# Attention rows split pair by pair, small loads on another queue, and a last block in two tiles

## The chip, the cores and the metric

The kernel runs on one core of one Trainium2 chip. The metric is the device time of one execution in microseconds. Before the change three runs took 2020.02, 2020.78 and 2021.38 us.

## The reference

The reference is an encoder trunk of two layers on x of 256 rows by 2048 columns, all in float32. Cut to what matters:

```
for l in range(DEPTH):
    h = rms_norm(x, norm1_g[l])
    q, k, v, gu, gv = jnp.split(h @ w_in[l], splits, axis=-1)
    q = apply_rope(rms_norm(q.reshape(B, S, N_Q_HEADS, HEAD_DIM), q_norm_g[l]), cos, sin)
    k = apply_rope(rms_norm(k.reshape(B, S, N_KV_HEADS, HEAD_DIM), k_norm_g[l]), cos, sin)
    attn = banded_window_attention(q, k, v, sink[l])
    sgu = chunked_spatial_gating(jax.nn.gelu(gu), jax.nn.gelu(gv), sgu_ln_g[l], sgu_ln_b[l], w_s[l], b_s[l])
    mixed = jnp.concatenate([rms_norm(attn, attn_out_g[l]), rms_norm(sgu, sgu_out_g[l])], axis=-1)
    x = x + mixed @ w_o[l]
    x = x + conv_gated_ffn(rms_norm(x, norm2_g[l]), w_up[l], conv_w[l], conv_b[l], w_down[l])
```

There are 8 query heads and 2 key heads of 128 columns, a gating unit of 1024 columns, and a feed-forward width of 5632.

## The kernel before, in words

**Products in three parts.** Every float32 factor is split into a high part (rounded to the matmul's fp32r type) and a low part (the rest). A product is high by high, high by low and low by high. `split_weights` (L112) asks for 1 MB of weights on SP's queue into one of three `raw` buffers; ScalarE copies a half of it (1024 columns) into one of four `hi` buffers (L128), and VectorE subtracts to one of four `lo` buffers (L110). Activations are split the same way into a `sl` tile of two parts: with a gain per row by `split_act` (ScalarE L246, VectorE L247), without one by `split_plain` or `parts` (L260, L261). `sl` tiles come from a pool of 43.

**Two forms of products.** `rows_by_cols` (L160) makes 256 rows by 512 columns of a result, in two halves `m` of 128 rows: 24 products of 512 columns for each 1 MB of weights (L166), six for each of four blocks of 128 rows of weights. `unit` (L187) makes columns by rows: 32 products of 512 (L202) and 32 of 256 columns (L207) for 2 MB. `pair` (L213) does this for two units of the feed-forward part (L225, L231). Results lie in PSUM: three `mm` tiles of two banks, and two `tp` tiles of one bank for transposes, scores and attention values.

**A layer.** First the keys, values and the first four query heads (`psk`, `psq`), four blocks of weights each; then `chunk(1)`, the second four query heads; `chunk(3)` and `chunk(4)`, the gating values; then four gating units (`gated`), the output projection (`out_rows`: four column blocks over the attention rows, four over the gating rows), and the feed-forward part in two halves of the width.

**The attention** is a Python generator, `attend` (L392), one for each group of four heads. Its steps are called between the weight blocks of the chunks, so that its small products stand among the large ones: rotation and norm of the queries; their transposes (L410); scores (L266 to L268 through `matmul3`), mask (L422), maximum and exp (L441); then for each pair of heads the scaling of the probabilities (L453), their transposes (L459), and the value product (L266 to L268 again). Its result is copied to an `sl` tile (L467) and its squares are added to `acca` (L277); the tile goes into a list `att`. After the first gating unit, L676 splits all eight rows of this list with the gain of the attention norm.

**What sets the order.** The code is written in the order of the work, and a scheduler moves instructions by priorities; `urgent()` puts weight splits and a few others ahead. Each engine then does its instructions in one fixed order, and waits at each for what it needs. `let_in` places the transposes of a norm (L320: the first norm `r1` as rows) behind 8 products of the block that runs then, and `tc.issue_after(latest())` lets nothing in it stand ahead of the instruction that was the latest of TensorE.

**The small loads.** In layer 0 the x rows that are split for the first products come on SP's queue between the weights, pair by pair (L515, `first_rows`). Ahead of the last block, x for the residual (`xr`, 2 MB in two loads, L554), the gains `qk`, the rest of the columns `pc` and `ropes` are asked for on SP's queue. The sum of squares of `xr` gives the first norm `r1` (L306, L310, L281, L283). In each layer `gating_tables` (L356) asks for two loads of `wsT` and six broadcasts of `prow` right after the first queries.

**Start and end.** `WARM` products of a tile of ones run ahead of the first weights (L97). The last column block of the last layer is added to the residual and stored from one `mm` tile: the weights' last 1 MB is run first for the one half of the rows, then for the other (`apart`), and L772 and L773 add and store one half whole and the other in two parts, on SP's queue.

Of the kernel before, what the change touches and what calls it, by code (L numbers as in the profile page):

```python
# [8 lines left out]
F32 = mybir.dt.float32  # L9
# [5 lines left out]
P = 128  # L15
# [15 lines left out]
WARM = 10  # L31
# [9 lines left out]
def encoder(ctx: ExitStack, tc: tile.TileContext, xT, x, w_in, w_gu, w_o, w_up, w_down, wsT, pcol, prow, rope, out):  # L41
# [106 lines left out]
    def latest():  # L148
        return next(i for i in reversed(nc.cur_bb.bb.instructions) if i.engine == mybir.EngineType.PE)
# [10 lines left out]
    def rows_by_cols(ps, acts, src, first, last, raw=None, apart=False):  # L160
        his, los = split_weights(src, raw)

        def product(m, kk, part):
            cs = slice(kk % 2 * W, (kk % 2 + 1) * W)
            w = (his if part < 2 else los)[kk // 2][:, cs]
            nc.tensor.matmul(  # L166
                ps[:, m, :], acts[kk][:, part % 2, m * P : (m + 1) * P], w,
                start=first and kk == 0 and part == 0, stop=last and kk == KB - 1 and part == 2,
            )

        if apart:
            for m in range(2):
                for kk in range(KB):
                    for part in range(3):
                        product(m, kk, part)
            return
        for kk in range(KB):
            for m in range(2):
                product(m, kk, 0)
                product(m, kk, 1)  # L180
            for m in range(2):
                product(m, kk, 2)
            if kk == 1:
                let_in()
# [207 lines left out]
    def attend(g, ps, r, kT, v, tab, qk, nsink, acc, outs):  # L392
# [55 lines left out]
        for pr in range(2):  # L448
# [20 lines left out]
            outs.append(o)  # L469
        yield  # L470


    def gained(tiles, g0, pc):
        return [split_act(t[:, i, :], pc[:, g0 + 2 * j + i : g0 + 2 * j + i + 1]) for j, t in enumerate(tiles) for i in range(2)]
# [48 lines left out]
    def residual(ps, c, r=None):  # L523
        with urgent():
            for m in range(2):
                to = xr[:, m, c * W : (c + 1) * W]
                if r is None:
                    nc.vector.tensor_tensor(out=to, in0=ps[:, m, :], in1=to, op=ALU.add)
                else:
                    nc.vector.scalar_tensor_tensor(  # L530
                        out=to, in0=ps[:, m, :], scalar=r[:, m : m + 1], in1=to, op0=ALU.mult, op1=ALU.add
                    )
# [4 lines left out]
    for l in range(DEPTH):  # L537
# [10 lines left out]
        for b in range(NB):  # L548
            if l == 0:
                first_rows(b)  # L550
            if b == NB - 1:
                if l == 0:
                    for m in range(2):
                        nc.sync.dma_start(xr[:, m, :], x[:, m, :])  # L554
# [7 lines left out]
            in_rows(psk, 2, b)  # L562
            in_rows(psq, 0, b)
        r1b = as_rows(r1)
        ws, lrows = gating_tables(l)
        acca = sl([P, 2, SEQ])
        att = []
# [26 lines left out]
        def chunk(c, steps):  # L594
            ps = mm()
# [4 lines left out]
            return ps  # L600

        def group_steps(g, ps):
            it = attend(g, ps, r1, kT, vs, tabs[0], qk, nsink, acca, att)
# [7 lines left out]
        second()  # L611

# [63 lines left out]
        atts = gained(att, C_AG, pc)  # L676
# [18 lines left out]
        def out_rows(half, c, r):  # L695
            ps = mm()
# [37 lines left out]
        for f0, f1 in ((0, 24), (24, NF)):  # L734
# [20 lines left out]
            for c in range(4):  # L755
                ps = mm()
                end = last and not more and c == 3
                for k in range(f0, f1, KB):
# [8 lines left out]
                for m in range(2):  # L767
                    step = W // 2 if end and m else W
                    for a in range(0, W, step):
                        to = xr[:, m, c * W + a : c * W + a + step]  # L770
                        with urgent():
                            nc.vector.tensor_tensor(out=to, in0=ps[:, m, a : a + step], in1=to, op=ALU.add)  # L772
                        nc.sync.dma_start(out[:, m, c * W + a : c * W + a + step], to)  # L773
# [57 lines left out]
```

## Time and profile before

| what | value |
|---|---|
| median of three runs | 2020.78 us |
| the profiled execution, its own time | 2020.79 us |
| its span | 2019.0 us |
| mean granted clock of TensorE | 0.998 |
| instructions | 26362 |
| DMA, mean | 189 GB/s |

The span is what the profiler saw, from the first to the last instruction; the execution's own time is 1.8 us longer. In the timeline a row has its start, its length, the engine, line and operation, out<-in, and the number of instructions merged; in brackets stands the idle time of the engine ahead of it and what ended it. PE is TensorE's products, PEld its weight loads, SPq and ACTq the queues' DMA issues. The lengths of overlapping instructions overlap, so the pitch of a merged row is what counts.

### The profile page before, as it was taken

To read this page: it belongs to the slowest core of one execution; us is meant where nothing else is said; L and a number is where in the kernel's file an instruction comes from. 1 tells how busy PE (TensorE), PEld (TensorE's weight loads), DVE (VectorE), ACT (ScalarE), POOL (GpSimd) and SP (SyncE) were. 2 spreads that over 40 slices of the span, in tenths; PEclk is the share of its full clock that TensorE was granted. 3 is DMA by queue.
4 is the path that set the end of the run, shared out by engine and by line. 5 is a ranking of instruction groups with operands and counts; after the bars stand their busy time and mean duration, and the time that the engine had idled before them with its cause. 6 is when DMAs were issued, how large, how long until landed. Compare 5 with 4: busy or idle time off the path is not lost.

```text
span 2019.0 us, 26362 instructions
## 1 busy us (share of the span) xinstructions
PE 2003.4 (99%) x10428; PEld 1719.2 (85%) x10428; DVE 1367.1 (68%) x1866; ACT 1066.3 (53%) x1459; POOL 19.2 (1%) x25
## 2 busy tenths in 40 slices
PE   9998999999999999999999999999999999999999
PEld 7787888888888888888888888888988888888887
DVE  6787666777765477776558696667777554777753
ACT  5665465555543365555445754655555434555542
POOL 0000000000000000000001000000000000000000
PEclk9999999999999999999999999999999999999999
DMA  8643554554565454456565445454555555455563
GB/s 325 236 137 135 188 167 167 212 186 167 205 215 193 164 209 182 167 211 209 186 230 184 149 157 197 158 198 167 188 210 199 195 194 182 167 191 206 209 210 124
DMA packets 58011, 382.22 MB, mean 189 GB/s; under 512 B 6688, under 2 KB 7968, under 8 KB 12832
## 3 DMA queue, kind: packets, MB, share of 16 engines
q1 hardware_dynamic: 57744, 380.53, 53.3%
q8 instruction: 81, 1.33, 0.3%
q14 instruction: 42, 0.34, 0.1%
q10 hardware_dynamic: 144, 0.02, 0.0%
HBM read 378.43 MB, written 2.10 MB: 188 GB/s over the span
## 4 chain that ended last, share of the span: by engine, by line
PE 93%; DVE 1%; ACT 0%; DMA 0%; issue 0%; POOL 0%; DVEq 0%; ACTq 0%; SPq 0%
PE mm L166 39%; PE mm L225 30%; PE mm L231 16%; PE mm L202 4%; PE mm L207 2%; DVE lo L110 1%; PE tp L501 1%; PE tp L266 0%; PE tp L648 0%; DMA raw<-in_w_up 0%; PE tp L268 0%; PE tp L267 0%; PE tp L459 0%; ACT hi L128 0%; DVE sl L261 0%
## 5 line engine op out<-in xcount | busy, mean ns | idle before, releaser
L110 DVE TENSOR_TENSOR lo<-raw,hi 128x1024 fp32r<-128x1024 f32 (+1 forms) x708 | 840.0, 1214 | 461.4 <-ACT hi L128 303.2
L128 ACT ACTIVATE hi<-raw 128x1024 fp32r<-128x1024 f32 (+1 forms) x708 | 732.6, 1051 | 683.4 <-PE mm L166 396.0
L166 PE MATMUL mm<-hi,sl 128*128 128x512 f32 x2560 | 692.9, 391 | 6.1 <-DVE sl L247 5.3
L225 PE MATMUL mm<-sl,hi 128*128 128x512 f32 x2688 | 617.5, 389 | 0.1
L225 PEld LDWEIGHTS mm<-sl,hi 128*128 128x128 f32 x2688 | 501.9, 188 | 103.0 <-ACT hi L128 0.5
L166 PEld LDWEIGHTS mm<-hi,sl 128*128 128x128 f32 x2560 | 478.9, 188 | 105.0 <-DVE sl L247 6.3
L166 PE MATMUL mm<-lo,sl 128*128 128x512 f32 x1280 | 395.8, 390 | 0.0
L231 PEld LDWEIGHTS mm<-sl,lo 128*128 128x128 f32 x2688 | 328.1, 192 | 3.3
L231 PE MATMUL mm<-sl,lo 128*128 128x256 f32 x2688 | 329.1, 283 | 0.0
L166 PEld LDWEIGHTS mm<-lo,sl 128*128 128x128 f32 x1280 | 240.4, 188 | 50.1
L726 DVE SCALAR_TENSOR_TENSOR sc<-ev,pc,sc 128x255 f32<-128x255 f32 x176 | 80.7, 480 | 87.9 <-ACT sc L725 87.9
L239 ACT COPY ev<-mm 128x512 f32<-128x512 f32 x96 | 55.4, 577 | 131.6 <-PE mm L231 114.8
L725 ACT ACTIVATE sc<-ev,pc 128x256 f32<-128x256 f32 x176 | 98.9, 589 | 0.0
L202 PE MATMUL mm<-sl,hi 128*128 128x512 f32 x384 | 92.4, 392 | 0.0
L202 PEld LDWEIGHTS mm<-sl,hi 128*128 128x128 f32 x384 | 70.9, 188 | 13.9
L729 DVE SCALAR_TENSOR_TENSOR sc<-ev,pc,sc 128x255 f32<-128x255 f32 x176 | 80.7, 480 | 3.0
L254 ACT ACTIVATE sl<-sl 128x256 fp32r<-128x256 f32 x88 | 31.8, 409 | 69.2 <-DVE sl L746 69.2
L241 DVE TENSOR_TENSOR ev<-mm,ev 128x512 f32<-128x512 f32 x96 | 65.4, 682 | 0.0
L721 DVE TENSOR_TENSOR ev<-ev,rb 128x512 f32<-128x512 f32 x88 | 59.9, 681 | 0.2
L207 PE MATMUL mm<-sl,lo 128*128 128x256 f32 x384 | 50.5, 284 | 0.0
L207 PEld LDWEIGHTS mm<-sl,lo 128*128 128x128 f32 x384 | 48.4, 191 | 1.0
L255 DVE TENSOR_TENSOR sl<-sl 128x256 fp32r<-128x256 f32 x88 | 33.4, 421 | 20.1 <-ACT sl L254 20.1
(117 smaller groups left out, 633.1 us busy)
## 6 DMA issues: line engine op xcount, KB each, us to landing
raw<-in_w_up SPq DMA_DIRECT2D x176, 1024.0 KB, 5.2
raw<-in_w_down SPq DMA_DIRECT2D x88, 1024.0 KB, 4.8
raw<-in_w_in SPq DMA_DIRECT2D x38, 1024.0 KB, 4.9
raw<-in_w_o SPq DMA_DIRECT2D x32, 1024.0 KB, 4.9
raw<-in_w_gu SPq DMA_DIRECT2D x16, 1024.0 KB, 4.9
sl<-in_prow SPq DMA_DIRECT2D x12, 256.0 KB, 5.7
raw<-in_w_in SPq DMA_DIRECT2D x8, 256.0 KB, 5.8
xr<-in_x SPq DMA_DIRECT2D x2, 1024.0 KB, 7.6
```

Source lines behind the costliest of these rows:

```text
L110: nc.vector.tensor_tensor(out=lo, in0=part, in1=hi.bitcast(F32), op=ALU.subtract)
L128: nc.scalar.activation(hi[:, cs], part, AF.Copy)
L166: nc.tensor.matmul(ps[:, m, :], acts[kk][:, part % 2, m * P : (m + 1) * P], w, start=first and kk == 0 and part == 0, stop=last and kk == ...
L202: nc.tensor.matmul(ps[:, i, :], tile_of(his, k, i), x1, start=k == 0, stop=False)
L207: nc.tensor.matmul(ps[:, i, :SEQ], tile_of(los, k, i), acts[k][:, 0, :], start=False, stop=k == NK - 1)
L225: nc.tensor.matmul(pss[n][:, i, :], hs[k // KB][:, c : c + P], x1, start=k == 0, stop=False)
L231: nc.tensor.matmul(pss[n][:, i, :SEQ], los[k // KB][:, c : c + P], acts[k][:, 0, :], start=False, stop=k == len(acts) - 1)
L241: nc.vector.tensor_tensor(out=s, in0=ps[:, :, :SEQ], in1=rest, op=ALU.add)
L721: nc.vector.tensor_tensor(out=s, in0=s, in1=r2b2[0], op=ALU.mult)
L725: nc.scalar.activation(t[:, i, :], s[:, i, :], AF.Identity, bias=col(3), scale=col(1))
L726: nc.vector.scalar_tensor_tensor(out=t[:, i, 1:], in0=s[:, i, : SEQ - 1], scalar=col(0), in1=t[:, i, 1:], op0=ALU.mult, op1=ALU.add)
L729: nc.vector.scalar_tensor_tensor(out=t[:, i, : SEQ - 1], in0=s[:, i, 1:], scalar=col(2), in1=t[:, i, : SEQ - 1], op0=ALU.mult, op1=ALU.add)
```

## The change

It has five parts.

- `attend` splits a pair of attention rows right where it has made them (L470 to L473 of before), with `gained`, and appends the split rows to `atts`; the splitting of all eight after the first gating unit is gone.
- In layer 0 the loads of `ropes`, `qk` and the rest of `pc` are issued from ScalarE's queue in the second block, and the two loads of `xr` in the third; each stands behind the instruction that was ScalarE's latest then.
- `gating_tables` is called after the first step of the second query group instead of ahead of the keys.
- The last column block gets two `tp` tiles of one bank, one for each half of the rows, and the store of the last 256 columns is issued from ScalarE's queue. For this `ps` is now a list of two halves in every caller.
- `WARM` is 9 instead of 10.

```
-WARM = 10
+WARM = 9
...
-    def attend(g, ps, r, kT, v, tab, qk, nsink, acc, outs):
+    def gained(tiles, g0, pc):
+        return [split_act(t[:, i, :], pc[:, g0 + 2 * j + i : g0 + 2 * j + i + 1]) for j, t in enumerate(tiles) for i in range(2)]
+
+    def attend(g, ps, r, kT, v, tab, qk, nsink, acc, pc, outs):
...
             add_squares(acc, o, g == 0 and pr == 0)
-            outs.append(o)
+            outs.extend(gained([o], C_AG + 4 * g + 2 * pr, pc))
...
                 first_rows(b)
+
+                with tc.issue_after(latest(mybir.EngineType.Activation)):
+                    if b == 1:
+                        ropes = const.tile([P, 2, 2, HD], F32, tag="ropes", name="ropes")
+                        nc.scalar.dma_start(ropes, rope)
+                        qk = layer_params_rest(0, pc, nc.scalar)
+                    if b == 2:
+                        for m in range(2):
+                            nc.scalar.dma_start(xr[:, m, :], x[:, m, :])
             if b == NB - 1:
                 if l == 0:
-                    for m in range(2):
-                        nc.sync.dma_start(xr[:, m, :], x[:, m, :])
                     for c in range(4):
                         sum_squares(ssq, c)
-                    qk = layer_params_rest(0, pc, nc.sync)
-                    ropes = const.tile([P, 2, 2, HD], F32, tag="ropes", name="ropes")
-                    nc.sync.dma_start(ropes, rope)
...
         r1b = as_rows(r1)
-        ws, lrows = gating_tables(l)
...
         second()
+        ws, lrows = gating_tables(l)
...
         gated(0)
-        atts = gained(att, C_AG, pc)
...
-                ps = mm()
                 end = last and not more and c == 3
+                ps = [tp([P, W]) for _ in range(2)] if end else (lambda t: [t[:, m, :] for m in range(2)])(mm())
...
-                        nc.sync.dma_start(out[:, m, c * W + a : c * W + a + step], to)
+                        (nc.scalar if end and a else nc.sync).dma_start(out[:, m, c * W + a : c * W + a + step], to)
```

The scheduler moves more than the diff says. SP's queue at the start, before (`raw` are weights, `sl<-in_xT` the x rows to be split, `xr` the residual's x):

```order
L118 DMA raw<-in_w_in 128x2048
L515 DMA sl<-in_xT 128x512
L118 DMA raw<-in_w_in 128x2048 x2
L515 DMA sl<-in_xT 128x512
L118 DMA raw<-in_w_in 128x2048
L515 DMA sl<-in_xT 128x512
```

and the same place after:

```order
L515 DMA sl<-in_xT 128x512
L118 DMA raw<-in_w_in 128x2048
L515 DMA sl<-in_xT 128x512
L118 DMA raw<-in_w_in 128x2048 x2
L515 DMA sl<-in_xT 128x512
L118 DMA raw<-in_w_in 128x2048
```

Each load of x rows now stands ahead of the weights that it stood behind.

TensorE between the transposes of the first group's queries (L410, in after L414; `ident` is the unit matrix) and its first scores (L266), before:

```order
L410 MATMUL tp<-ident,sl 128x128 x4
L166 MATMUL mm<-hi,sl 128x512 x2
L166 MATMUL mm<-lo,sl 128x512 x2
L166 MATMUL mm<-hi,sl 128x512 x4
L266 MATMUL tp<-sl 128x256
```

and after:

```order
L414 MATMUL tp<-ident,sl 128x128 x8
L166 MATMUL mm<-hi,sl 128x512 x4
L166 MATMUL mm<-lo,sl 128x512 x2
L166 MATMUL mm<-hi,sl 128x512 x4
L166 MATMUL mm<-lo,sl 128x512 x2
L166 MATMUL mm<-hi,sl 128x512 x4
L166 MATMUL mm<-lo,sl 128x512 x2
L166 MATMUL mm<-hi,sl 128x512 x4
L166 MATMUL mm<-lo,sl 128x512 x2
L266 MATMUL tp<-sl 128x256
```

Eight products stood between them, and 24 do now.

VectorE ahead of layer 0's output projection, before (L241 and L638 join and scale a gating unit, L277 adds squares, L247 splits, L288 and L296 sum the attention's squares):

```order
L110 TENSOR_TENSOR lo<-raw,hi 128x1024 x3
L241 TENSOR_TENSOR ev<-mm,ev 128x512
L110 TENSOR_TENSOR lo<-raw,hi 128x1024
L638 TENSOR_TENSOR ev<-ev,rb 128x512
L277 TENSOR_TENSOR sl<-sl,sc 128x512
L247 SCALAR_TENSOR_TENSOR sl<-sl,pc 128x256 x8
L288 TENSOR_TENSOR sl<-sl 128x256
L296 TENSOR_REDUCE as<-tp 128x2
```

and after (L643 is L638 of before):

```order
L643 TENSOR_TENSOR ev<-ev,rb 128x512
L277 TENSOR_TENSOR sl<-sl,sc 128x512
L247 SCALAR_TENSOR_TENSOR sl<-sl,pc 128x256 x2
L261 TENSOR_TENSOR sl<-tp,sl 128x512 x2
L277 TENSOR_TENSOR sl<-sl,sc 128x512
L288 TENSOR_TENSOR sl<-sl 128x256
L247 SCALAR_TENSOR_TENSOR sl<-sl,pc 128x256
L296 TENSOR_REDUCE as<-tp 128x2
L247 SCALAR_TENSOR_TENSOR sl<-sl,pc 128x256
```

The eight splits in a row are gone; those of the last two pairs are left here, two behind the one sum, and one each around the sums for the norm.

More of the change, by code (lines that the diff above doesn't have):

```diff
@@ L145, in split_later, with latest @@
         return los
-    def latest():
-        return next(i for i in reversed(nc.cur_bb.bb.instructions) if i.engine == mybir.EngineType.PE)
+    def latest(engine=mybir.EngineType.PE):
+        return next(i for i in reversed(nc.cur_bb.bb.instructions) if i.engine == engine)
     waiting = []
@@ L166, in product @@
             nc.tensor.matmul(
-                ps[:, m, :], acts[kk][:, part % 2, m * P : (m + 1) * P], w,
+                ps[m], acts[kk][:, part % 2, m * P : (m + 1) * P], w,
                 start=first and kk == 0 and part == 0, stop=last and kk == KB - 1 and part == 2,
@@ L468, in attend @@
             add_squares(acc, o, g == 0 and pr == 0)
-            outs.append(o)
+            outs.extend(gained([o], C_AG + 4 * g + 2 * pr, pc))
         yield
-    def gained(tiles, g0, pc):
-        return [split_act(t[:, i, :], pc[:, g0 + 2 * j + i : g0 + 2 * j + i + 1]) for j, t in enumerate(tiles) for i in range(2)]
     qk = None
@@ L550, in encoder @@
                 first_rows(b)
+                with tc.issue_after(latest(mybir.EngineType.Activation)):
[6 more added lines that the diff above has]
+                            nc.scalar.dma_start(xr[:, m, :], x[:, m, :])
             if b == NB - 1:
                 if l == 0:
[L553 to L554 removed]
                     for c in range(4):
                         sum_squares(ssq, c)
[L557 to L559 removed]
                 tabs, nsink = rope_tables(qk, ropes)
                 r1 = inv_rms_rows(ssq, "x")
[L562 to L563 removed]
+            in_rows([psk[:, m, :] for m in range(2)], 2, b)
+            in_rows([psq[:, m, :] for m in range(2)], 0, b)
         r1b = as_rows(r1)
[L565 removed]
         acca = sl([P, 2, SEQ])
[L567 removed]
+        atts = []
         kms = st([P, 2, 2], "kms")
@@ L594, in chunk @@
         def chunk(c, steps):
-            ps = mm()
+            t = mm()
+            ps = [t[:, m, :] for m in range(2)]
             for b in range(NB):
@@ L599, in chunk @@
                     step()
-            return ps
+            return t
         def group_steps(g, ps):
-            it = attend(g, ps, r1, kT, vs, tabs[0], qk, nsink, acca, att)
+            it = attend(g, ps, r1, kT, vs, tabs[0], qk, nsink, acca, pc, atts)
             return lambda: next(it)
@@ L695, in out_rows @@
         def out_rows(half, c, r):
-            ps = mm()
+            t = mm()
+            ps = [t[:, m, :] for m in range(2)]
             for b in range(2):
```

7 lines of the change are left out of this document (3 added, 4 removed).

## Prediction

> **What bounds the kernel now.** I read the page first, its busy times and the chain that ended last.
>
> ```profile
> PE 2003.4 (99%) x10428; PEld 1719.2 (85%) x10428; DVE 1367.1 (68%) x1866; ACT 1066.3 (53%) x1459; POOL 19.2 (1%) x25
> PE 93%; DVE 1%; ACT 0%; DMA 0%; issue 0%; POOL 0%; DVEq 0%; ACTq 0%; SPq 0%
> 1253.20 10.93 PE mm L166 x48
> ```
>
> TensorE is busy for 2003.4 of the span's 2019.0 us and holds 93% of the chain. A weight product of 512 columns takes 10.93 / 48 = 0.228 us (the third line, from the chain in order of time). The change removes one tiny warm-up product and no other, so it can only move the places where TensorE stands still. So I went through the timeline of PE alone, from start to end, for rows that begin with an idle time:
>
> ```profile
> 9.40 1.20 PE L166 MATMUL mm<-hi,sl 128*128 128x512 f32 x4 [0.77 <-ACT hi L128]
> 59.62 0.43 PE L320 MATMUL tp<-ident,xr 128*128 128x128 f32 x2 [0.74 <-POOL xr L283]
> 95.34 0.38 PE L266 MATMUL tp<-sl 128*128 128x256 f32 x1 [1.05 <-DVE sl L261]
> 105.28 0.36 PE L266 MATMUL tp<-sl 128*128 128x256 f32 x1 [1.41 <-DVE sl L422]
> 135.97 0.66 PE L459 MATMUL tp<-ident,sl 128*128 128x128 f32 x4 [0.23 <-DVE sl L261]
> 189.92 1.65 PE L166 MATMUL mm<-hi,sl 128*128 128x512 f32 x3 [5.30 <-DVE sl L247]
> 1165.98 0.47 PE L266 MATMUL tp<-sl 128*128 128x512 f32 x1 [0.40 <-DVE sl L261]
> ```
>
> All but the last lie in layer 0, and one is larger than all others together. It also costs more than its length, as the view by windows shows (after the engines' busy times come the granted clock, the DMA share and GB/s):
>
> ```profile
> 190.00:192.00 2.00, 2.00 (x5) 1.61 (x6) 2.00 (x6) 0.00 (x0) 0.00 (x0) 0.50 0.91 377
> 192.00:193.60 1.60, 1.60 (x6) 0.97 (x6) 0.97 (x3) 0.00 (x0) 0.00 (x0) 0.50 0.26 108
> 193.60:195.00 1.40, 1.40 (x14) 1.40 (x14) 0.87 (x3) 0.00 (x0) 0.47 (x1) 0.97 0.00 0
> ```
>
> After the pause TensorE runs at half clock from 189.92 to 193.60, so 3.68 x 0.5 = 1.8 us are lost on top. The shorter pauses are not followed by this.
>
> **Part 1, the attention splits.** What TensorE waited for at 189.92 is all eight splits in one row:
>
> ```profile
> 183.04 3.50 DVE L110 TENSOR_TENSOR lo<-raw,hi 128x1024 fp32r<-128x1024 f32 x3 [5.24 <-ACT hi L128]
> 183.18 1.69 ACT L246 ACTIVATE sl<-sl,pc 128x256 fp32r<-128x256 f32 x4
> 184.23 0.39 PE L166 MATMUL mm<-hi,sl 128*128 128x512 f32 x1
> 189.40 3.24 DVE L247 SCALAR_TENSOR_TENSOR sl<-sl,pc 128x256 fp32r<-128x256 f32 x8
> ```
>
> The chain in order of time has the price of the gating unit's half-length products:
>
> ```profile
> 1293.15 3.83 PE mm L207 x32
> ```
>
> TensorE was at the output projection at 184.23, but VectorE had stood idle for 5.24 us and then did low weight parts, a join and a sum first. A split of one pair costs ScalarE 2 x 1.69 / 4 = 0.85 us and VectorE 2 x 3.24 / 8 = 0.81 us. After the change three pairs are split long before, and only the last pair's two stand near the projection; by the order of VectorE they come ahead of the gating's sums. Between the last pair's value product and the projection TensorE has 4 big and 32 half-length products, 4 x 0.228 + 3.83 = 4.7 us, and the projection's first 24 products read the other group's pairs, 5.5 us more. In these 10.2 us ScalarE has a copy, a square, a high weight part and two splits to do, and VectorE two sums and two splits; at no more than 1.06 us each for the first three (the length of a high part, in a row below) that is 3.2 + 0.85, and 0.4 for the last split, 4.4 us. So the pause goes: 5.3 + 1.8 = **7.1 us**. If the cover failed, 7.1 would come back.
>
> What is put ahead of something else: each pair's 0.85 and 0.81 us stand before the next pair's copies and low parts, for which TensorE waits (the rows at 95.34, 135.97 and 1165.98 are this kind of wait). Between the first transposed probabilities and the first value product TensorE now has 8 products in layer 0 and 7 in layer 1, where it had 11 and 14: 1.8 and 1.6 us. Per place I bound the wait by 0 (the copies land in time) and 1.41 (the largest such row); four first pairs make 0 to 5.6. The two waits nearest to this in kind took 0.23 and 0.40, so I take 0.25 for each place, **1.0 us** in all, and count those two old waits as staying.
>
> **Part 2, the small loads.** Today the residual x is asked for on SP's queue, between weight loads:
>
> ```profile
> 42.38 0.42 SPq L554 DMA_DIRECT2D xr<-in_x  x1
> 57.08 0.62 ACT L306 ACTIVATE sc<-xr 128x512 f32<-128x512 f32 x1
> 57.60 0.19 ACT L306 ACTIVATION_READ_ACCUMULATOR sc<-xr 128x1 f32 x1
> 58.86 0.71 POOL L283 TENSOR_TENSOR xr<-xv,mhalf 128x2 f32<-128x2 f32 x1 [56.63 <-DVE xv L281]
> ```
>
> Its second half is asked for at 42.38, so the last square ends at 57.79 and the norm at 59.57, and the transposes of L320 wait 0.74. Now ScalarE asks for x one block of 48 products, 10.9 us, earlier in the program. The scheduler put L320's transposes after 204 products in place of 227: from 17.69 (48 products done) that is 17.69 + 156 x 0.228 = 53.3. The last two squares stand behind a high part whose buffer frees 38 products before its own use, about product 178, 47.3 us; with 1.06 for the part, two squares at 0.62 + 0.19 and the 1.8 from the last square to the norm that it took before, it is ready near 51.8. Gain **0.7**.
>
> The early norm moves what follows. Between the queries' transposes and the first scores stand 24 products, not 8: the 1.05 wait needed 8 x 0.228 + 1.05 = 2.9 us and gets 5.5. Between those and the third score stand 61, not 30: needed 6.8 + 1.41 = 8.2, given 13.9. Gain **2.5**.
>
> Against it: each of five loads takes ScalarE about 0.42 us of issue, and other loads meet them.
>
> ```profile
> 50.53 1.06 ACT L128 ACTIVATE hi<-raw 128x1024 fp32r<-128x1024 f32 x1 [1.66 <-PE mm L166]
> raw<-in_w_in SPq DMA_DIRECT2D x38, 1024.0 KB, 4.9
> xr<-in_x SPq DMA_DIRECT2D x2, 1024.0 KB, 7.6
> ```
>
> ScalarE waits 1.66 us before each high part because the buffer isn't free, not for the load; that hides 0.42 us each, and the 36 products of buffers ahead hide more. An x load of 1 MB beside a weight load of 1 MB took 7.6 where 4.9 is usual, so I bound the delay by 2.7 us per half, 5.4 in all, and take 0. The Trainium skill ("DMA: Bandwidth & Descriptors", section "Issuing engines are not separate DMA queues") says that all queues feed the same 16 DMA engines, so a second queue adds no bandwidth; by it alone x would hold back a weight load as before, and the sum would lose up to those 5.4 us if no cover stood there.
>
> The gating tables go behind the second queries' weights, past eight weight loads of 24 products each at the most:
>
> ```profile
> 59.79 0.65 SPq L364 DMA_DIRECT2D sl<-in_prow  x1
> 135.83 0.68 DVE L667 TENSOR_TENSOR vn<-vn,sl 128x512 f32<-128x512 f32 x1
> ```
>
> Asked for from 59.79 + 8 x 5.5 = 104 on, they are there long before their first reader at 135.83: nothing, and the weight loads that they stood before come a little sooner, into full buffers.
>
> **Part 3, the start.**
>
> ```profile
> 1.05 4.63 PE L97 MATMUL tp<-ones 128*128 128x128 f32 x20 [1.05 <-DVE ones L93]
> 5.34 1.46 PE L166 MATMUL mm<-hi,sl 128*128 128x512 f32 x4
> 8.71 0.63 ACT L128 ACTIVATE hi<-raw 128x512 fp32r<-128x512 f32 x1 [1.07 <-DMA raw<-in_w_in]
> 12.71 0.63 ACT L128 ACTIVATE hi<-raw 128x512 fp32r<-128x512 f32 x1 [0.36 <-DMA raw<-in_w_in]
> 15.30 1.06 ACT L128 ACTIVATE hi<-raw 128x1024 fp32r<-128x1024 f32 x1 [1.95 <-DMA raw<-in_w_in]
> 16.33 1.07 PE L166 MATMUL mm<-hi,sl 128*128 128x512 f32 x4
> 17.69 1.36 PE L166 MATMUL mm<-hi,sl 128*128 128x512 f32 x4
> ```
>
> One warm-up product of ten (two passes of twenty) is 0.46 us. The first real product, at 5.34, can come that much earlier, but the third piece of weights lands at 8.71 whatever TensorE does, and the start at 9.40 stays: nothing. The Trainium skill ("TensorE: Matmul & The Clock Gate", section "Part 1: The HAM clock gate (the "warmup" mystery)") says that the clock starts at half and rises after some 3.4 us of activity, whatever the number of products; if the shorter warm-up missed that window, the twelve products before 9.40 at double length would take 5.5 us from 4.9 and end at 10.4, a loss of 1.0 us by estimate. The sum goes by the rows: nothing.
>
> Then SP asks for the second pair of x rows (0.25 MB) ahead of the next weights. 1 MB took 15.30 - 12.71 = 2.6 us, so the weights land 0.65 later, at 15.95, and their high part ends at 17.0, before TensorE asks at 17.69. In return these x rows are split before they are needed: the four products at 17.69 took 1.36 us against the usual 1.07, and the next x rows can do the same once more. Gain **0.4** of the 0.3 to 0.6; if the weights came after 17.69 instead, the end is a loss of as much.
>
> **Part 4, the end.**
>
> ```profile
> 2011.31 0.39 PE L166 MATMUL mm<-lo,sl 128*128 128x512 f32 x1
> 2014.45 1.35 DVE L772 TENSOR_TENSOR xr<-mm,xr 128x512 f32<-128x512 f32 x3 [9.02 <-PE mm L166]
> 2015.17 1.31 SPq L773 DMA_DIRECT2D out_x<-xr  x3
> L772 DVE TENSOR_TENSOR xr<-mm,xr x9: 414/680/692, 1932.9 to 2015.4; 128x512 f32<-128x512 f32 x7, 128x256 f32<-128x256 f32 x2
> L773 SPq DMA_DIRECT2D out_x<-xr x9: 332/343/446, 1933.6 to 2016.0; - x9
> DMA to landing us min/median/max: 1.9/2.1/2.1
> ```
>
> The first half of the rows is done at 2011.70 but is added only at 2014.45, since both halves are one tile. In two tiles it is added and stored beside the second half's products. Then two halves of 0.414 us, overlapping to 0.34 apart, end at 2015.20, and the last store starts at 2015.24 on ScalarE's queue, not at 2016.0: **0.7 us**. If a store from that queue landed later, 0 to 0.7.
>
> **The sum.** 7.1 + 0.7 + 2.5 + 0.4 + 0.7 - 1.0 = 10.4 us. The profiled execution took 2020.79, its span 2019.0 and 1.8 around it; the median of the runs is 2020.78, the same. Forecast **2010.4 us**.
>
> **The rivals.** (1) *The hand-offs eat a part.* With 7 and 8 products of cover, each of the four first pairs waits 1.0 to 1.4 us: 3 to 4.6 more than I took, 2013.4 to 2015. For it: the rows at 95.34 and 105.28; against: the copies are ordered right behind the transposes. (2) *The projection still pauses.* Something else at the end of VectorE's row, such as the last pair, holds it for 5.30 and the clock halves: 7.1 back, 2017.5, no change that can be told. (3) *Slower.* The pause that halves the clock moves into the hand-offs: VectorE, held by a low part that waits for its buffer as it was for 5.24 us, lets TensorE stand long enough there. Each is worth 7.1; two cancel the gain (2024.6), from three on it is slower: 2031.7. Against it, no hand-off paused over 1.41. (4) *The early x holds back weights* at the start, against full buffers: 5.4 at most, 2013 to 2015.8.
>
> **Chances.** About 0.2%, 4 us, is what a measurement of this kernel can tell from no change: faster is below 2016.8, slower above 2024.8. Forecast 0.62; (1) 0.14; (4) 0.06; (2) 0.10; (3) 0.04; 0.04 unnamed, half of it faster, half the same. Faster 0.84, same 0.12, slower 0.04. The range goes from all waits gone (the sum without the 1.0 and with 0.23 and 0.40 gone too: 2008.8, less 0.3 for spread) to the ends of (1) and (4): **2008.5 to 2016.0**.
>
> **What would show it.** Right: no idle time over 1 us before a product of L166 near 180 us and a granted clock of 1.00 there; no wait at L320; scores without waits of 1.05 and 1.41; the last store starting near 2005 and 0.7 us sooner after the last product. Wrong: rows of L266 or of the probabilities' transposes with idle times over 1 us, in layer 1 above all, or a high part that waits for DMA between 20 and 50 us and a product that waits for it.

## The result, and the profile after

The changed kernel takes 2008.41 us (median of 6 runs, 2008.03 to 2008.88), the kernel before 2020.33 (6 runs, 2019.68 to 2021.38): a ratio of 0.9941, 95% interval 0.9928 to 0.9954. The gain is 11.9 us where 10.4 were forecast, and the time lies 0.09 below the low end of the range. The profiled execution took 2008.75, its span 2007.0, so the two spans differ by 12.0.

The page's busy times and the chain that ended last, of the changed kernel:

```profile
PE 2000.7 (100%) x10426; PEld 1718.6 (86%) x10426; DVE 1367.1 (68%) x1866; ACT 1068.1 (53%) x1460; POOL 20.4 (1%) x25
PE 97%; DMA 2%; DVE 1%; issue 0%; ACT 0%; SPq 0%; POOL 0%; DVEq 0%; ACTq 0%
```

These are its rows of PE with an idle time ahead of them, from start to end, and the view by windows of the stretch that had the pause:

```profile
42.14 1.48 PE L166 MATMUL mm<-hi,sl 128*128 128x512 f32 x4 [0.65 <-ACT sl L246]
137.22 0.39 PE L266 MATMUL tp<-sl 128*128 128x256 f32 x1 [0.21 <-DVE sl L426]
177.49 0.41 PE L294 MATMUL tp<-ident,sl 128*128 128x128 f32 x2 [0.16 <-DVE sl L288]
1158.63 1.25 PE L463 MATMUL tp<-ident,sl 128*128 128x128 f32 x8 [0.40 <-DVE sl L457]
126.00:200.00 74.00, 73.62 (x420) 64.17 (x419) 63.31 (x109) 48.85 (x80) 1.39 (x2) 1.00 0.42 143
```

The pause of 5.30 us is gone, with the waits at L320, at the scores (1.05, 1.41) and at 9.40; the granted clock is 1.00. New are a wait for x rows at 42.14 and two short ones. Idle time ahead of PE's rows, as the profile lists it, fell from 10.95 to 2.48 us, 1.05 of it ahead of the first product in both.

The transposes of a norm (L320) stand four times in TensorE's order and make milestones. These are the last three before, then all four after:

```profile
300.27 0.38 PE L320 MATMUL tp<-ident,yr 128*128 128x128 f32 x2
1064.49 0.38 PE L320 MATMUL tp<-ident,xr 128*128 128x128 f32 x2
1299.57 0.38 PE L320 MATMUL tp<-ident,yr 128*128 128x128 f32 x2
```

```profile
53.44 0.38 PE L320 MATMUL tp<-ident,xr 128*128 128x128 f32 x2
288.42 0.38 PE L320 MATMUL tp<-ident,yr 128*128 128x128 f32 x2
1052.64 0.38 PE L320 MATMUL tp<-ident,xr 128*128 128x128 f32 x2
1288.23 0.38 PE L320 MATMUL tp<-ident,yr 128*128 128x128 f32 x2
```

The first of them stands 23 products (5.2 us) earlier in the order than before, so 5.2 is added to it and taken from the stretch behind it:

| stretch | before | after | difference | forecast |
|---|---|---|---|---|
| start to first norm | 59.62 | 58.65 | -1.0 | -1.1 (0.7 + 0.4) |
| to layer 0's second norm | 240.65 | 229.8 | -10.9 | -9.1 (7.1 + 2.5 - 0.5) |
| to layer 1's first norm | 764.22 | 764.22 | 0 | 0 |
| to layer 1's second norm | 235.08 | 235.59 | +0.5 | +0.5 |
| to the last product's end | 714.85 | 715.10 | +0.25 | 0 |
| to the span's end | 4.58 | 3.67 | -0.9 | -0.7 |

The end of the changed kernel, in the timeline:

```profile
2000.65 0.69 DVE L777 TENSOR_TENSOR xr<-tp,xr 128x512 f32<-128x512 f32 x1 [6.29 <-PE tp L166]
2002.94 0.39 PE L166 MATMUL tp<-lo,sl 128*128 128x512 f32 x1
2003.37 0.76 DVE L777 TENSOR_TENSOR xr<-tp,xr 128x256 f32<-128x256 f32 x2 [2.03 <-PE tp L166]
2004.15 0.35 ACTq L778 DMA_DIRECT2D out_x<-xr  x1
```

The first half is added while the second is multiplied, and the last store starts 0.8 us behind the last product's end at 2003.33, where it was 1.6 behind before.

### The profile page after: what moved, and what is told of

Same layout as the page of the kernel before. It is cut to its first block, busy times and chain, and to the rows that moved or that the text cites. A ratio compares the mean times of both kernels' runs of the same rounds, so it can differ in the third digit from the quotient of the medians.

```text
span 2007.0 us, 26356 instructions
## 1 busy us (share of the span) xinstructions
PE 2000.7 (100%) x10426; PEld 1718.6 (86%) x10426; DVE 1367.1 (68%) x1866; ACT 1068.1 (53%) x1460; POOL 20.4 (1%) x25
## 4 chain that ended last, share of the span: by engine, by line
PE 97%; DMA 2%; DVE 1%; issue 0%; ACT 0%; SPq 0%; POOL 0%; DVEq 0%; ACTq 0%
PE mm L166 40%; PE mm L225 30%; PE mm L231 16%; PE mm L202 4%; PE mm L207 2%; PE tp L166 1%; DMA raw<-in_w_in 1%; PE tp L501 1%; DMA sl<-in_xT 1%; PE tp L463 0%; PE tp L266 0%; PE tp L653 0%; DVE lo L110 0%; PE tp L268 0%; PE tp L267 0%
## 5 line engine op out<-in xcount | busy, mean ns | idle before, releaser
L166 PE MATMUL mm<-hi,sl 128*128 128x512 f32 x2480 | 668.0, 391 | 0.7 <-ACT sl L246 0.7
L166 PEld LDWEIGHTS mm<-hi,sl 128*128 128x128 f32 x2480 | 463.9, 188 | 96.4 <-ACT sl L246 1.1
L166 PE MATMUL mm<-lo,sl 128*128 128x512 f32 x1240 | 382.9, 390 | 0.0
L166 PEld LDWEIGHTS mm<-lo,sl 128*128 128x128 f32 x1240 | 232.5, 188 | 48.1
L241 DVE TENSOR_TENSOR ev<-mm,ev 128x512 f32<-128x512 f32 x96 | 65.7, 684 | 0.0
```

Of the source, the lines that this page charges most:

```text
L166: nc.tensor.matmul(ps[m], acts[kk][:, part % 2, m * P : (m + 1) * P], w, start=first and kk == 0 and part == 0, stop=last and kk == KB - 1 ...
L241: nc.vector.tensor_tensor(out=s, in0=ps[:, :, :SEQ], in1=rest, op=ALU.add)
```

## The experiments

The theory to test is the forecast's own: the splits by pairs remove the pause, the earlier loads remove the waits at L320 and at the scores, the tables do nothing. The rival is that one wait has several removers among the parts, so that their gains don't add.

**The parts one at a time.** The splits alone, put into the kernel before:

```
-            outs.append(o)
+            outs.extend(gained([o], C_AG + 4 * g + 2 * pr, pc))
...
-        atts = gained(att, C_AG, pc)
```

> The kernel before with one part of the change alone: each pair of attention rows is split where it is made. Theory A: the pause of 5.30 us near 185 us goes with its 1.8 us of halved clock, and up to 0.4 us of new waits at the hand-offs comes: 2020.3 - 7.1 + 0.4 = 2013.6 us, 2013.0 to 2014.2; the other waits (0.77, 0.74, 1.05, 1.41) stay. Rival B (the other parts made the gain): 2018 to 2020. Rival C (with the transposes where they were, the hand-offs have less cover and wait 1.0 us each at four places): 2015 to 2017.

Measured: 2013.92 us (2013.60 to 2015.17; before on the same chip 2020.46), ratio 0.9969 (0.9958 to 0.9981): 6.5 less. A holds. The pause is gone, the score waits stay, and the hand-offs take more in layer 1:

```profile
94.75 0.39 PE L266 MATMUL tp<-sl 128*128 128x256 f32 x1 [1.02 <-DVE sl L261]
104.67 0.36 PE L266 MATMUL tp<-sl 128*128 128x256 f32 x1 [1.41 <-DVE sl L426]
1151.79 1.22 PE L463 MATMUL tp<-ident,sl 128*128 128x128 f32 x8 [0.78 <-DVE sl L457]
```

The tables alone:

```
-        ws, lrows = gating_tables(l)
         acca = sl([P, 2, SEQ])
...
         second()
+        ws, lrows = gating_tables(l)
```

> The kernel before with the gating tables alone asked for behind the second queries. In TensorE's order the scores stand further behind the transposes than before, but the last pair's value product stands where it stood. Theory A (the pause comes from eight splits in one row right behind a late last pair; the earlier loads or the splits remove it, the tables don't): the waits of 1.05 and 1.41 go, the pause of 4 to 6 us and the halved clock stay: 2020.4 - 2.5 = 2017.9 us, 2017.2 to 2018.8. Rival B (the tables' 2 MB in the sl pool and SP's queue held everything back, the pause too): 2010.5 to 2012.

Measured: 2017.30 us (2016.16 to 2018.14; before 2020.56), ratio 0.9984 (0.9975 to 0.9992): 3.3 less. A holds, and "nothing" was wrong: the score waits went with the tables' place alone. In its timeline a shorter wait comes at 133.93, and the pause is there as before, with half the granted clock behind it (third row, by windows):

```profile
133.93 0.50 PE L266 MATMUL tp<-sl 128*128 128x512 f32 x1 [0.52 <-DVE sl L261]
185.77 1.65 PE L166 MATMUL mm<-hi,sl 128*128 128x512 f32 x3 [5.31 <-DVE sl L247]
185.77:188.00 2.23, 2.23 (x5) 1.82 (x6) 2.23 (x6) 0.00 (x0) 0.00 (x0) 0.50 0.91 364
```

The small loads alone:

```
+                with tc.issue_after(latest(mybir.EngineType.Activation)):
+                    if b == 1:
...
+                        qk = layer_params_rest(0, pc, nc.scalar)
+                    if b == 2:
+                        for m in range(2):
+                            nc.scalar.dma_start(xr[:, m, :], x[:, m, :])
...
-                        nc.sync.dma_start(xr[:, m, :], x[:, m, :])
```

> The kernel before with the small loads alone put on ScalarE's queue, earlier in the program. In TensorE's order the first norm's transposes stand 5.3 us earlier, and the last value product of the attention about 18 us earlier, one to two gating units ahead of where it stood, so that the eight splits in one row no longer stand close before the projection. Theory A (an early last pair removes the pause as well as the splits do): no pause over 1 us near 185 us, 2020.4 - 7.1 - 0.7 = 2012.6 us; the scores stand close behind the transposes still, so of their 2.5 us 0 to 2.5 go, and of the start's stall 0 to 1: 2009.5 to 2012.8. Rival B (it takes the splits or the tables): the pause stays, 2016.5 to 2019.7.

Measured: 2009.87 us (2009.19 to 2010.65; before 2020.56), ratio 0.9947 (0.9933 to 0.9960): 10.7 less. A holds: neither the pause nor the score waits are there, though the splits stand in one row. In TensorE's order only 6 weight products stand between the queries' transposes and the first scores here, so it isn't distance between these two that spared the wait. What is late now are the keys' transposes:

```profile
69.21 0.30 PE L595 MATMUL tp<-ident,sl 128*128 128x128 f32 x1 [0.96 <-DVE sl L584]
```

The three gains add up to 20.5 us; all together, with the end and the warm-up, give 12. They remove the same waits.

**One part undone.** The changed kernel with the splits in one row after the first gating unit:

```
-            outs.extend(gained([o], C_AG + 4 * g + 2 * pr, pc))
+            outs.append(o)
...
         gated(0)
+        atts = gained(att, C_AG, pc)
```

> The changed kernel with one part undone: the eight attention rows are split in one row after the first gating unit, as before. Theory A (the splitting in one row made the pause at the projection): a pause of 4 to 6 us stands again before a product of L166 near 180 us, followed by 3 to 4 us at half the granted clock; the new small waits at the hand-offs (0.22 and 0.16) go. 2008.4 + 5.3 + 1.8 - 0.4 = 2015.1 us, 2014 to 2016. Rival B (the earlier norm and the tables' later place already gave VectorE its 5 us back, so that the splits only look guilty): a pause under 1.5 us and no halved clock, 2008.2 to 2010.

Measured: 2007.98 us (2007.18 to 2008.87; before 2020.46), ratio 0.9939 (0.9927 to 0.9952). Theory A falls: no pause, and no time lost. Its rows, on ScalarE, VectorE and TensorE, and then the copy of the last pair in the kernel before:

```profile
163.06 0.57 ACT L471 COPY sl<-tp 128x512 f32<-128x512 f32 x1
173.16 3.25 DVE L247 SCALAR_TENSOR_TENSOR sl<-sl,pc 128x256 fp32r<-128x256 f32 x8
183.21 1.09 PE L166 MATMUL mm<-hi,sl 128*128 128x512 f32 x4
```

```profile
179.29 0.57 ACT L467 COPY sl<-tp 128x512 f32<-128x512 f32 x1
```

With the norm and the tables moved, the last pair is made 16 us earlier, so the eight splits, still in one row, end at 176.4, ahead of the projection at 183.2. Before, they ran from 189.40 to 192.64 with the projection already at 184.23. The pause needed both: a row of eight and a late last pair. The changed kernel itself is another case: its last pair is copied only 4.4 us earlier than before, and no more than that pair's splits are left then, done well ahead of the projection (the copy, the last split and the projection's first products):

```profile
174.91 0.59 ACT L471 COPY sl<-tp 128x512 f32<-128x512 f32 x1 [1.21 <-PE tp L268]
178.28 0.48 DVE L247 SCALAR_TENSOR_TENSOR sl<-sl,pc 128x256 fp32r<-128x256 f32 x1
182.68 1.09 PE L166 MATMUL mm<-hi,sl 128*128 128x512 f32 x4
```

The small loads back on SP's queue, ahead of the last of the first blocks:

```
-                            nc.scalar.dma_start(xr[:, m, :], x[:, m, :])
...
+                        nc.sync.dma_start(xr[:, m, :], x[:, m, :])
```

> The changed kernel with the residual x, the gains and the rope rows asked for as before, on SP's queue ahead of the last of the first blocks; the gating tables stay late. Theory A (the loads' place set the norm, the scores and the start): the waits of L320 (0.74) and of the scores (1.05 and 1.41) are back, 3.2 us, and so is the start's 1.15 us (a stall near 9.4 and slow products near 17.7), while the new wait of 0.66 us at 42 goes: 2008.4 + 3.2 + 1.15 - 0.66 = 2012.1 us, 2011.5 to 2012.7. Rival B (the start's gain is the shorter warm-up's, or chance): no stall near 9.4, 2010.9. Rival C (the scores' waits went with the splits or the tables): 2009 to 2009.6.

Measured: 2009.46 us (2009.14 to 2009.67; before 2020.46), ratio 0.9946 (0.9933 to 0.9958). C holds: L320's wait is back, those at the scores are not.

```profile
7.09 1.20 PE L166 MATMUL mm<-hi,sl 128*128 128x512 f32 x4 [0.64 <-ACT hi L128]
58.78 0.43 PE L320 MATMUL tp<-ident,xr 128*128 128x128 f32 x2 [0.74 <-POOL xr L283]
135.78 0.50 PE L266 MATMUL tp<-sl 128*128 128x512 f32 x1 [0.62 <-DVE sl L261]
```

The tables back ahead of the keys:

```
-        ws, lrows = gating_tables(l)
...
+        ws, lrows = gating_tables(l)
         acca = sl([P, 2, SEQ])
```

> The changed kernel with one part undone: the gating tables are asked for ahead of the keys again. Theory A (the tables' place gave the scores their distance): one or two waits of 0.5 to 1.5 us at the scores (L266) between 80 and 110 us, no pause at the projection: 2008.2 + 1 to 2.5 = 2009.2 to 2010.7 us. Rival B (the earlier norm alone does that, as the forecast counted it): 2007.8 to 2008.7, no such wait.

Measured: 2009.88 us (2009.61 to 2010.33; before 2020.56), ratio 0.9948 (0.9935 to 0.9960). The time is A's, the rows are not: no wait at the scores, but 0.96 at the keys' transposes (as with the loads alone), and 0.78 in place of 0.40 in layer 1. So the tables' place is worth about 1.5 us beside the other parts.

The end in one tile again:

```
-                ps = [tp([P, W]) for _ in range(2)] if end else (lambda t: [t[:, m, :] for m in range(2)])(mm())
+                ps = (lambda t: [t[:, m, :] for m in range(2)])(mm())
```

> The changed kernel with the last column block in one tile again (the last store stays on ScalarE's queue). Theory A (both halves are one tile, so the first is added only when the second is done): the first addition at the end waits for the last product and three additions stand in a row, so that the span's end comes 0.3 to 0.5 us later (of the 0.7 to 0.9 the other 0.4 is the second queue's): 2008.2 + 0.4 = 2008.6 us. Rival B (the end is set by the last store's landing alone): 2008.0 to 2008.3, and the last store starts no later behind the last product.

Measured: 2009.21 us (2007.77 to 2011.18; before 2020.56), ratio 0.9944 (0.9932 to 0.9957), too wide for a term of this size. The trace tells it:

```profile
2001.08 0.39 PE L166 MATMUL mm<-lo,sl 128*128 128x512 f32 x1
2001.51 1.35 DVE L777 TENSOR_TENSOR xr<-mm,xr 128x512 f32<-128x512 f32 x3 [9.01 <-PE mm L166]
2002.89 0.35 ACTq L778 DMA_DIRECT2D out_x<-xr  x1
```

From the last product's end (2001.47) to the span's end (2006.0) it takes 4.5 us, as before (4.58), against 3.67 in two tiles. The 0.9 is the two tiles'; ScalarE's queue for the last store adds nothing that shows. A had the direction right, but only half of the size.

Ten warm-up products:

```
-WARM = 9
+WARM = 10
```

> The changed kernel with ten warm-up products in place of nine. Theory A (the start hangs on when the third piece of weights lands, and that on what else was asked for): the first product of weights comes 0.43 us later, but the thirteenth still near 8.65, no stall: 2008.4 us, 2008.1 to 2008.7. Rival B (the shorter warm-up moved the start): everything 0.4 to 0.5 us later, 2008.9. Rival C (the landing is a matter of chance from run to run): the third piece's high part starts anywhere from 7.6 to 8.7 and a stall of up to 0.8 us may be back in the profiled run, with no steady difference in the median.

Measured: 2007.90 us (2007.67 to 2008.97; before 2020.46), ratio 0.9939 (0.9925 to 0.9952). A holds: the first product comes at 5.34 in place of 4.91, the thirteenth at 8.88 in place of 8.65, and the time is the same.

**The price of the halved clock.** In the kernel before, TensorE is kept busy through most of the pause:

```
         def out_rows(half, c, r):
             ps = mm()
+            if l == 0 and half == 0 and c == 0:
+                with tc.issue_after(latest()), urgent():
+                    for _ in range(22):
+                        nc.tensor.matmul(ps[:, 0, :P], ones, ones, start=True, stop=True)
```

> The kernel before, with 22 products of a tile of ones put ahead of the output projection of layer 0, so that TensorE is busy for some 4.8 us of its pause of 5.3 us (they are overwritten by the products that follow). Theory A (the pause costs its length and, after it, a halved clock, 1.8 us on the big products and more on the small ones): the granted clock stays 1.00 after the pause, and the time falls by 1.8 to 2.4 us: 2020.5 - 2.1 = 2018.4 us. Rival B (the halved clock after the pause has another cause, or costs nothing): 2020.2 to 2020.9, the half clock still there. Rival C (the products take longer than the pause): up to 1 us more than A.

Measured: 2017.89 us (2017.29 to 2018.25; before 2020.63), ratio 0.9987 (0.9978 to 0.9996): 2.7 less, by more work. The added products, the projection and, by windows, the clock:

```profile
182.72 5.07 PE L700 MATMUL mm<-ones 128*128 128x128 f32 x44
188.42 0.96 PE L166 MATMUL mm<-hi,sl 128*128 128x512 f32 x3 [0.40 <-DVE sl L247]
189.90:193.60 3.70, 3.70 (x23) 3.03 (x21) 3.27 (x8) 1.06 (x1) 0.00 (x0) 1.00 0.27 115
```

A holds on the clock, which stays 1.00; the time fell by a little more than A's 2.4. The stretch between the first and the second norm takes 238.90 in place of 240.65, 1.75 less, where the forecast had 1.8. The rest of the 2.7 lies outside this stretch, and its cause stays open.

**Traces repeated, and a better place for x.** The changed kernel once more, unedited:

> The changed kernel once more, as a second trace of the same program beside the next three. Theory A (the start, the x rows' lateness near 42 us and the last 700 us differ from run to run, the rest doesn't): median 2007.9 to 2008.6 us; the waits of 0.2 near 137 and 177 us and of 0.39 near 1158 us stand again to 0.02 us, the wait near 42 us is anything from 0 to 0.9, the first stall-free block of weights ends within 0.3 us of where it did, the last 715 us vary by 0.2 to 0.6. Rival B (a program's trace repeats to 0.1 us everywhere, so that every row of the first trace can be read as the change's): the wait near 42 us is 0.66 again.

Measured: 2008.22 us (2007.08 to 2009.18; before 2020.63), ratio 0.9939 (0.9926 to 0.9951). A holds. The waits near 137, 177 and 1158 stand again within 0.03 us; that near 42 is 0.26 now, and one is new:

```profile
41.84 1.48 PE L166 MATMUL mm<-hi,sl 128*128 128x512 f32 x4 [0.26 <-ACT sl L246]
1697.99 7.32 PE L225 MATMUL mm<-sl,hi 128*128 128x512 f32 x31 [0.55 <-ACT hi L128]
```

The kernel before once more, unedited, in one execution:

> The kernel before once more, for a second trace of it. Theory A (its first trace had a slow start by chance, the rest repeats): the first norm's transposes stand at 58.2 to 59.2 us instead of 59.62, the stretch from there to the second norm's transposes is 240.65 us again within 0.1, with the pause of 5.3 us and the waits of 1.05 and 1.41. Rival B (the start's 0.77 us at 9.40 belongs to the old order of the loads): 59.5 to 59.8, with a stall of 0.7 to 0.8 at 9.4.

Measured: one execution of 2021.20 us. The first norm's transposes stand at 59.10, the next at 300.07: 240.97 for the stretch, with a pause of 5.31 and score waits of 1.02 and 1.41. The stall of the start is another one, beside that of the loads alone (the second row, of that run):

```profile
17.53 0.96 PE L166 MATMUL mm<-hi,sl 128*128 128x512 f32 x3 [0.42 <-DVE sl L247]
```

```profile
9.35 1.19 PE L166 MATMUL mm<-hi,sl 128*128 128x512 f32 x4 [0.98 <-ACT hi L128]
```

So the stall at 9.40 is not tied to the old order of loads: it is away in this trace of the old order and there in one of the new. A holds on that; the repeat within 0.1 was too strict, it is 0.3.

The wait near 42 us, in the first trace of the changed kernel, comes from x rows that were asked for at 31.38 and on which ScalarE, waiting for them, began at 41.58:

```profile
31.38 0.43 SPq L515 DMA_DIRECT2D sl<-in_xT  x1
32.91 0.33 ACTq L559 DMA_DIRECT2D xr<-in_x  x1
41.58 0.91 ACT L246 ACTIVATE sl<-sl,pc 128x256 fp32r<-128x256 f32 x2 [4.89 <-DMA sl<-in_xT]
```

So the second half of x was asked for one block later:

```
-                    if b == 2:
-                        for m in range(2):
-                            nc.scalar.dma_start(xr[:, m, :], x[:, m, :])
+                    if b >= 2:
+                        nc.scalar.dma_start(xr[:, b - 2, :], x[:, b - 2, :])
```

> The changed kernel with the second half of the residual x asked for one block later, still on ScalarE's queue. Theory A (both halves of x beside the weights held back the x rows of the last block, 10.2 us from issue to landing, and with them the high parts and TensorE near 42 us): the wait near 42 us is gone, and the first norm's transposes wait no longer than 0.3 us: 2007.9 us, 2007.4 to 2008.3. Rival B (the second half, late, holds the norm back): a wait of 0.5 to 2 us at L320, 2008.5 to 2010.

Measured: 2008.60 us (2008.17 to 2012.25; before 2020.63), ratio 0.9945 (0.9932 to 0.9957). B holds: nothing near 42, but 0.83 at L320. That a trace shows no wait near 42 proves little by itself: of the seven traces that ask for both halves of x early, five have one (0.20 to 0.93 us) and two (the end in one tile, the splits in one row) have none. The x rows say more. In each of the seven, ScalarE waits for them until 9.7 to 10.3 us after their issue; with the second half later, in this run and in the next, it doesn't wait for them.

The same with the splits in one row:

> The changed kernel with the splits in one row again, and the second half of the residual x asked for one block later. Theory A (with the loads and the tables moved, the splits by pairs are worth nothing in layer 0 and cost 0.4 us in layer 1; spreading x takes the wait for x rows near 42 us away): 0.4 us less than the changed kernel without them, and 0 to 0.9 for the other: 2007.4 us, 2007.0 to 2007.9, no wait near 1158 us. Rival B (splits in one row cost VectorE's row something elsewhere): 2008.4 or more, and some wait over 0.5 us between 150 and 190 us or in layer 1.

Measured: 2007.81 us (2007.21 to 2008.63; before 2020.63), ratio 0.9936 (0.9923 to 0.9950). It is the lowest median, 0.4 below the changed kernel on the same chip, but the two ranges overlap. The traces tell more: layer 1's stretch between its norms takes 235.16 and 235.11 us in the two traces with the splits in one row, and 235.59 to 235.67 in five of the changed order. That the splits by pairs cost 0.5 us there, and gain nothing beside the other parts, is shown by the traces, not by the medians.

**Changes between small and large products.** In the stretch of 10.9 us, waits fell by 7.6 us (7.99 to 0.37) and the clock gave 1.8. That leaves 1.5 us in rows with no recorded wait. TensorE changes between weight products and small ones 66 times there before and 54 times after, so each change might cost something by itself. Two kernels have 192 small products more, in rows of 32 or singly; this is the edit of the second:

```
             for k in range(len(acts)):
                 for i in range(2):
...
                     nc.tensor.matmul(pss[n][:, i, :], hs[k // KB][:, c : c + P], x1, start=k == 0, stop=False)
+                    if small_ones:
+                        nc.tensor.matmul(pss[1][:, 0, :P], ones, ones, start=True, stop=True)
```

> The changed kernel with 192 products of a tile of ones more, in six of the feed-forward pairs of layer 0: ahead of the 32 weight products of a pair stand 32 of them in a row (they are overwritten by the products that follow). It is the yardstick of the next run, with the same work and 12 changes between the two kinds. At 0.22 us for one (5.07 / 22 us, two passes): 2008.3 + 192 x 0.22 = 2050 us, 2047 to 2053.

> The same 192 products, now one behind each of the 32 weight products, 384 changes between small and large products in place of 12. Theory A (each change costs TensorE some time that no wait shows; a lone large product between small ones took 0.32 us instead of 0.23): 372 x 0.045 = 17 us more than the run with them in rows, 10 to 25; what the change gained without a recorded wait, about 1 us on 12 changes fewer, would by itself want 0.08 for each, 31 us. Rival B (changes cost nothing, the rest of the gain lies elsewhere): within 3 us of the other run.

Measured: 2051.32 us in rows (2050.68 to 2051.85; before 2020.37, ratio 1.0153, 1.0138 to 1.0168) and 2052.03 singly (2051.86 to 2053.53, ratio 1.0158, 1.0141 to 1.0175). 0.7 us for 372 changes is 0.002 each. B holds: the change by itself is free. Singly, then in a row:

```profile
299.88 0.48 PE L228 MATMUL mm<-sl,hi 128*128 128x512 f32 x1
300.20 0.38 PE L230 MATMUL mm<-ones 128*128 128x128 f32 x2
300.33 0.48 PE L228 MATMUL mm<-sl,hi 128*128 128x512 f32 x1
```

```profile
296.38 7.30 PE L226 MATMUL mm<-ones 128*128 128x128 f32 x64
```

One of each takes 300.33 - 299.88 = 0.45 us, and 7.30 / 32 + 0.23 is 0.46.

**Where the 1.5 us are.** The starts of the rows tell. A product of 512 columns stands in its row with 0.39 us, but the next one can start 0.23 us behind it. So the idle time listed behind such a product is 0.16 us shorter than what TensorE lost: the pause is 189.92 - 184.23 - 0.23 = 5.46 us by its starts, where 5.30 is listed. A short delay isn't listed at all, as in these two rows of the kernel before, whose starts are 0.49 us apart:

```profile
132.75 0.47 PE L202 MATMUL mm<-sl,hi 128*128 128x512 f32 x1
133.24 0.66 PE L410 MATMUL tp<-ident,sl 128*128 128x128 f32 x4
```

Now take every product of the stretch between layer 0's norms, from its start to the next one's, and add up what goes over the usual for its size by more than 0.04 us. That makes 14.5 us before and 3.5 after (15.0 and 3.5 in the second traces), the halved clock included. The difference is 11.0 us, and the stretch gained 10.9. So the 1.5 us are delays too: some 0.3 hidden behind listed waits, and 1.2 in delays too short to be listed. What each of the short ones waited for is not shown.

## Why the prediction was right, and where it failed

**The pause, 7.1.** The size was right: the clock's 1.8 measured 1.75, the pause repeats at 5.30 to 5.31, and the splits alone give 6.5 with some 0.5 of new waits against them (0.33 for 0.23, 0.78 for 0.40). The cause was half the story. TensorE went on at 189.92, half a microsecond into the row of eight, so it did not wait for all eight, as the prediction read it, but for VectorE to reach the first. And either part removes the pause: the splits by pairs do with the loads back in their old place, and with the splits in one row the earlier loads do, by making the last pair 16 us earlier. In the changed kernel neither is needed beside the other. The Trainium skill ("TensorE: Matmul & The Clock Gate", section "Part 1: The HAM clock gate (the "warmup" mystery)") says that the clock goes back to half after at least one idle window of about 3.4 us. The traces agree: 5.30 and 5.31 us of pause are followed by a granted clock of 0.50, 1.41 and 0.40 are not.

**The waits at L320 and the scores, 0.7 and 2.5.** They went, as forecast, but at the scores not for the reason given. The prediction put the 24 products ahead of the first scores down to the early norm. The loads alone leave 6 there and the tables alone 8, as before, and neither run has the waits of 1.05 and 1.41. The tables' place, counted as nothing, is worth 3.3 us alone in the median (2.4 of it between layer 0's norms) and 1.5 beside the rest. The prediction looked at SP's queue for it; the traces show another order of work. With the tables late, the first of the keys' transposes stands 37 weight products behind the norm's in place of 99, and the third score 82 behind the ones before it in place of 30. Which of these changes spared which wait is not shown.

**The start, 0.4.** Nothing of it shows. Brought to the same product and without L320's own wait, the first norm's transposes stand at 57.4 to 58.9 us in six traces with the old order of loads and at 57.4 to 59.1 in nine with the new. The prediction read one trace's stalls (9.40, 17.69) as the program's. That the table has -1.0 up to the first norm, near the forecast -1.1, is luck: 0.7 is L320's, and the second traces of the two kernels have 0.7 in all. WARM, counted as nothing, was right.

**The x loads on a second queue, 0 of up to 5.4.** Rival 4 came true in small: 0.65, 0.26 and 0.93 us of waiting near 42 in the first trace, in the second and in that with ten warm-ups. With x asked for later the x rows no longer come late, at the price of L320's wait (0.83 and 0.47).

**The hand-offs, 1.0.** Near: one wait of 0.2 in layer 0, where an old one of 0.23 went, and 0.5 us in layer 1's stretch. No hand-off paused for over 0.4 us, so rivals 1 and 3 did not come, nor did rival 2's pause at the projection.

**The end, 0.7.** It measured 0.9, and came from the two tiles.

**The step that failed** is how standing still was priced: "So I went through the timeline of PE alone, from start to end, for rows that begin with an idle time". That the change "can only move the places where TensorE stands still" was right, but the listed idle times are not all of it. In the stretch between layer 0's norms the listed waits and the clock gave 9.4 us, near the forecast 9.1; from start to start TensorE lost 11.0 less. These other 1.5 us were in no term, neither of the sum nor of the low end of the range, which took all listed waits as gone. Counted by parts and not by places, 1.5 us is also what the tables' place, a term put at nothing, is worth beside the rest; the two are not separate gains.

By how little the time missed the range, 0.09 us, is chance. The range stands on 2020.78, the median of three runs; six runs have 2020.33, 0.45 lower.

## What to carry to other kernels

When several edits act on one order of work, price each part alone and undone before crediting it: here three parts gained 6.5, 3.3 and 10.7 us alone and 12 together. A pause at a late consumer has two ends, the work done just before it and the time at which its input was made; ask for both what would have to move. Read stalls in the first 20 us, and terms under a microsecond, from several traces, and price a wait from start to start of the products, since the listed idle time leaves out a part of it and all of the short delays.

## What the runs showed of the hardware

- A pause of TensorE of 5.3 us was followed by half the granted clock in each of the three traces that had it, and filling it with 22 small products kept the clock at 1.00 and made the kernel 2.7 us faster in the median, 1.75 of it in the stretch that holds the pause.
- 0.25 MB of x rows on SP's queue took 9.7 to 10.3 us in seven traces, from issue until ScalarE could begin on them, while two 1 MB loads stood on ScalarE's queue; with one of the two later ScalarE did not wait for them. The Trainium skill ("DMA: Bandwidth & Descriptors", section "Issuing engines are not separate DMA queues") says that DMAs of all issuing engines interleave on the same 16 engines; these rows agree.
- The granted clock reads 1.00 over the first 5 us, though a pass of the warm-up takes 4.63 / 20 = 0.23 us there and one of the same kind 7.30 / 64 = 0.11 near 300 us. The start's slowness has to be read from the products.
- 372 changes between 128-column and 512-column products that wait for nothing cost 0.7 us in all.
- A product of 512 columns is listed with 0.39 us but followed by the next 0.23 us behind its start, so a delay of up to 0.16 us behind it shows no idle time.
- Two traces of the same program agree to 0.04 us in most waits. The first norm stands 0.3 (after) and 0.5 us (before) apart in them, and the last 715 us differ by 0.7 and 0.5 (714.5 to 715.9 over all the traces), where a high part now and then waits for its weights.
